# Pacing the conditioning projection of a two-layer hybrid transformer by stage instead of at one rate

## The chip, the cores and the metric

The kernel runs on one core of one Trainium2 chip. The metric is device time in microseconds, from the first to the last instruction with what lies around them. The median of 3 runs of the kernel before is 2766.06 us (2765.82 to 2766.23).

## The reference: what is computed

Two layers of a transformer backbone run over 512 latent tokens and 128 context tokens, which share all weights. Cut to what matters here, one layer is:

```python
sh1, sc1, gt1, sh2, sc2, gt2 = split(silu(c) @ w_mod[l] + b_mod[l], 6)      # adaLN: c for latents, c_ctx for context
h  = rmsnorm(x, norm1_g[l]) * (1 + sc1) + sh1
z  = h @ w_in[l] + b_in[l]                       # q, k, v of four mixers, and the branch gates
o  = [natten(z), dense_gqa(z), windowed_gqa(z), mlstm(z)]                   # mixers A, B, C, D
x  = x + gt1 * ((sum_i sigmoid(gate_i) * (o[i] @ w_branch[l, i])) @ w_out[l])
h2 = rmsnorm(x, norm2_g[l]) * (1 + sc2) + sh2
g, u = split(h2 @ w_ffn_in[l], 2)
x  = x + gt2 * ((silu(g) * u) @ w_ffn_out[l])
# after both layers: one final rmsnorm
```

D_MODEL is 1024, D_FF 2816. The adaLN projection `silu(c) @ w_mod[l]` has 6144 outputs for each of two conditioning vectors; `w_mod` is 25 MB for each layer.

## The kernel before, in words

**Tiling.** The 640 tokens lie side by side. `hT` holds the normed activations transposed, in two fp32r parts (high and low), and every float32 product is three TensorE matmuls: L414, L415, L416 in `mm3`, L1803 to L1805 in the paired part of the feed-forward. Weights come as 128x1024 blocks through SyncE's queue into two `raw` tiles (L397); ScalarE casts the high part `whi` (L402) and VectorE subtracts for the low part `wlo` (L403), into rings of five.

**Stages of a layer.** `mixers` runs projections and attention of A, D, B, C, and after each mixer its branch merge M0, M3, M1, M2 (`merge`, L1596 to L1610); while M2 runs (M20 to M23), no attention runs any more. Then come the output projection with its gated residual (`residual_tm`, L1631 and L1632), and, in `norm_tm`, the last two of its four column groups token tile by token tile, each followed by the next norm: sums of squares (L635 to L639), the root on GpSimd (L644), scaling (L649), TensorE transposes (L657), the modulation on ScalarE and VectorE, and the two parts of `hT` (L669, L670; the second half's low part on GpSimd). The feed-forward has four plain blocks (L1900, L1903) and then 18 paired ones (`ff_pair`), in four groups, each group followed by its output projection (`fo`) and residual. Group 3 ends in the norm of the next layer.

**The background.** Of the 24 column chunks of `w_mod` (12 for each layer, 512 columns each), `start` computes chunks 0 to 3 of layer 0 in the foreground, since the first norm needs them. The other 20 are the generator `adaln_all`. A chunk is eight accumulation steps: a 128x512 block of `w_mod` is loaded into one of four `wm` tiles (L497), VectorE multiplies and adds it into `msum` for the first vector (L477 for the first step, then L479), ScalarE multiplies it for the second (L473) and GpSimd adds that (L475; none in a chunk's first step). Then four transposes for each vector (L486) and a reduction (L487) give columns; for the chunks of the gates there is a second transpose (L516), a copy (L517) and a DMA to DRAM (L519).

**What sets the order.** Whenever a foreground generator has issued some matmuls, `run` or `drive` calls `tick`, which adds `bg[0]` to a credit and lets `adaln_all` go on for each whole step in it. `bg[0]` is `BGRATE` = 0.2 from the end of `start` to the end of the kernel. `bg_until` runs the rest of what is needed in one go where a stage needs certain chunks. The code order gives priorities; a scheduler then puts the instructions of each engine into one fixed order, by its own simulated times, and each engine executes its order strictly.

```python
    def tick():
        bg[1] += bg[0]
        bg_steps(int(bg[1]))
        bg[1] -= int(bg[1])
```

Of the kernel before, what the change touches and what calls it, by code (L numbers as in the profile page):

```python
# [86 lines left out]
BGRATE = 0.2  # L87
# [137 lines left out]
def trunk(ctx: ExitStack, tc: tile.TileContext, a: dict, depth: int):  # L225
    nc = tc.nc
# [240 lines left out]

    def adaln_acc(accs, w, kk, tmp=None):

        for v in range(2):  # L470
            s = csil[:, kk, v:v + 1]
            if v and tmp is not None:
                S.activation(accs[v][:, :512] if kk == 0 else tmp, w, AF.Copy, scale=s)  # L473
                if kk:
                    G.tensor_tensor(accs[v][:, :512], accs[v][:, :512], tmp, ALU.add)  # L475
            elif kk == 0:
                V.tensor_scalar(accs[v][:, :512], w, s, None, ALU.mult)  # L477
            else:
                V.scalar_tensor_tensor(accs[v][:, :512], w, s, accs[v][:, :512], ALU.mult, ALU.add)  # L479

# [10 lines left out]
    def adaln_all(items):  # L491


        def load(x):
            if x < KT * len(items):
                (l, ch), k = items[x // KT], x % KT
                SY.dma_start(wm_tiles[x % 4], a["w_mod"][l, P * k:P * k + P, 512 * ch:512 * ch + 512])  # L497

# [34 lines left out]
    def start():  # L533
# [49 lines left out]
        for x, ch in enumerate(order):  # L583
# [21 lines left out]
            for k in range(k0, k0 + 4):  # L605
                z = xT[k // 2][:, NTOK * (k % 2):NTOK * (k % 2) + NTOK]
                h = f640()
                for v, c0, c1 in ((0, 0, NS), (1, NS, NTOK)):
                    S.activation(h[:, c0:c1], z[:, c0:c1], AF.Identity, bias=modc[:, 1, v, k:k + 1],
                                 scale=modc[:, 0, v, k:k + 1])  # L610
                V.tensor_copy(hT[:, k, 0, :], h)
                V.tensor_tensor(hT[:, k, 1, :], h, hT[:, k, 0, :].bitcast(F32), ALU.subtract)
        for pl, t in held:
            pl.give(t)
        bigs.give(big)
        ms.give(*xT)
        bg[0] = BGRATE
# [1032 lines left out]
    def drive(bulk, streams):  # L1650
# [22 lines left out]
        for name, needs, rate, gen in bulk:  # L1673
            if any(n not in done for n in needs):
                flush()
# [17 lines left out]
    def mixers(l, d, *start):  # L1693
        done.clear()

# [145 lines left out]
    def layer(l, *start):  # L1841
# [20 lines left out]
        bg_until(l, *range(6, 10))  # L1862
        hook = norm_tm(xs, pieces, KT, mg_lhs, gts, ms, 1)
# [11 lines left out]
        for g, cnt in enumerate(FF_SPLIT):  # L1875
# [4 lines left out]
            for jx in range(cnt):  # L1880
# [13 lines left out]
                if j >= FF_PLAIN:  # L1894
                    run(ff_pair(ops, ff_load(l, j, spare, ts), at))
                    continue
# [17 lines left out]
                if j == FF_PLAIN - 1:  # L1914
                    for k in range(4):
                        split(hT[:, k, 0, HALF:], hT[:, k, 1, HALF:], s1[:, HALF * k:HALF * k + HALF])
                    qs.give(s1)
# [14 lines left out]
            if g < 3:  # L1932
                for n in range(4):
                    residual_tm(xs, fo(n), cnt, lhs, gts, n)
            else:
                pieces = {0: fo(0), 1: fo(1), **pieces}
                hook = norm_tm(xs, pieces, cnt, lhs, gts, ks, 0 if l + 1 < depth else None)
# [102 lines left out]
```

## Time and profile before

| | us | share of the span |
|---|---|---|
| median of 3 runs | 2766.06 | |
| the profiled execution (span 2761.6 us) | 2763.34 | |
| TensorE (PE) busy | 2677.5 | 97% |
| VectorE (DVE) busy | 2126.9 | 77% |
| ScalarE (ACT) busy | 1432.3 | 52% |
| GpSimd (POOL) busy | 743.1 | 27% |

Busy time is an average over stages. The rows further down take single stretches: a `--windows` row gives, for a stretch, its length, each engine's busy time and its count of instructions, the granted TensorE clock (1.00 is all of 2.4 GHz, 0.50 is 1.2 GHz), the share of the DMA engines and GB/s. A timeline row gives start, duration, engine, line, operation, output and input tiles, shapes and count; in brackets how long the engine sat idle before it and what ended that.

### The profile page before, as it was taken

How to read it: one execution, taken by the hardware profiler on the slowest of the kernel's cores; microseconds unless marked ns; L12 is line 12 of the kernel's file. 1: busy time of each engine (PE TensorE's matmuls, PEld its weight loads, DVE VectorE, ACT ScalarE, POOL GpSimd, SP SyncE). 2: the span in 40 equal slices, each digit the busy share in tenths (PEclk: the TensorE clock that was granted, in tenths of full speed). 3: DMA queues.
4: the chain of work that ended last, by engine and by line, in shares of the span. 5: the costliest groups of instructions: out<-in, count | busy, mean ns of one | idle time of the engine just before them, and what ended most of it. 6: DMA issues, size and time to landing. Idle time of an engine off the chain costs nothing.

```text
span 2761.6 us, 51944 instructions
## 1 busy us (share of the span) xinstructions
PE 2677.5 (97%) x19514; PEld 2626.9 (95%) x19514; DVE 2126.9 (77%) x4780; ACT 1432.3 (52%) x3298; POOL 743.1 (27%) x650
## 2 busy tenths in 40 slices
PE   7999999999999899999989999999999999999998
PEld 4998999999999899999989999999999999999998
DVE  7767768888973787888877867778888847586967
ACT  5865446666652543434458744456666535333433
POOL 2001112121142435365440101212112332243433
PEclk9999999999999999999999999999999999999999
DMA  8223323112243333333332323312122432222222
GB/s 286 91 87 115 97 79 98 47 56 79 62 124 114 100 111 104 92 108 108 96 118 90 124 89 114 93 56 77 56 75 66 123 123 70 92 77 85 81 93 73
DMA packets 123580, 264.28 MB, mean 96 GB/s; under 512 B 14193, under 2 KB 40145, under 8 KB 123329
## 3 DMA queue, kind: packets, MB, share of 16 engines
q1 hardware_dynamic: 123328, 260.97, 29.8%
q8 instruction: 153, 2.51, 0.4%
q14 instruction: 99, 0.80, 0.1%
HBM read 252.73 MB, written 7.95 MB: 94 GB/s over the span
## 4 chain that ended last, share of the span: by engine, by line
PE 76%; DVE 12%; ACT 4%; issue 4%; DMA 2%; POOL 2%; SPq 0%; DVEq 0%; POOLq 0%; ACTq 0%
PE acc L414 17%; PE acc L415 17%; PE acc L416 17%; PE acc L1803 3%; PE acc L1804 3%; PE acc L1805 3%; PE O L1224 2%; PE T L1214 2%; DVE msum L479 2%; DVE wlo L403 1%; PE O L1804 1%; PE O L1803 1%; PE O L1805 1%; DMA raw<-wflat 1%; DMA wm<-w_mod 1%
## 5 line engine op out<-in xcount | busy, mean ns | idle before, releaser
L414 PE MATMUL acc<-hT,whi 128*128 128x384 f32 (+1 forms) x2240 | 701.3, 315 | 21.0 <-DVE hT L669 9.5
L415 PE MATMUL acc<-hT,whi 128*128 128x384 f32 (+1 forms) x2240 | 700.8, 313 | 6.0 <-DVE hT L670 4.2
L416 PE MATMUL acc<-hT,wlo 128*128 128x256 f32 (+1 forms) x2240 | 696.6, 312 | 1.1 <-DVE wlo L403 1.1
L402 ACT CAST whi<-raw 128x512 fp32r<-128x512 f32 (+1 forms) x488 | 299.5, 619 | 403.1 <-PE acc L415 186.4
L403 DVE TENSOR_TENSOR wlo<-raw,whi 128x512 fp32r<-128x512 f32 (+1 forms) x488 | 373.2, 768 | 136.4 <-ACT whi L402 129.2
L414 PEld LDWEIGHTS acc<-hT,whi 128*128 128x128 f32 x2240 | 424.1, 190 | 27.9 <-DVE hT L669 10.6
L415 PEld LDWEIGHTS acc<-hT,whi 128*128 128x128 f32 x2240 | 425.2, 190 | 9.4 <-DVE hT L670 5.0
L416 PEld LDWEIGHTS acc<-hT,wlo 128*128 128x128 f32 x2240 | 424.5, 190 | 2.3 <-DVE wlo L403 1.3
L475 POOL TENSOR_TENSOR msum<-msum,mtmp 128x512 f32<-128x512 f32 x140 | 214.9, 1535 | 262.6 <-ACT msum L473 164.7
L1604 POOL TENSOR_TENSOR m<-m,f 128x256 f32<-128x256 f32 x96 | 100.1, 1046 | 521.9 <-DVE f L1602 319.7
L1632 POOL TENSOR_TENSOR big<-big,t 128x256 f32<-128x256 f32 x150 | 128.5, 866 | 248.3 <-DVE t L1631 239.7
L729 ACT CAST pth<-T 128x512 fp32r<-128x512 f32 (+1 forms) x232 | 118.1, 521 | 103.3 <-PE T L1214 58.2
L473 ACT ACTIVATE mtmp<-wm,csil 128x512 f32<-128x512 f32 x140 | 101.2, 723 | 127.5 <-POOL msum L475 123.2
L730 DVE TENSOR_TENSOR ptl<-T,pth 128x512 fp32r<-128x512 f32 (+1 forms) x232 | 137.1, 601 | 37.2 <-ACT pth L729 36.0
L1631 DVE TENSOR_TENSOR t<-acc,P 128x256 f32<-128x256 f32 x200 | 82.8, 419 | 107.6 <-PE acc L416 84.8
L451 ACT CAST whi<-of 128x512 fp32r<-128x512 f32 x144 | 88.9, 620 | 146.2 <-PE acc L1804 47.6
L414 PE MATMUL acc<-whi,m 128*128 128x256 f32 x560 | 158.3, 284 | 4.7 <-DVE t L1631 4.5
L414 PE MATMUL acc<-big,whi 128*128 128x256 f32 (+1 forms) x512 | 158.7, 311 | 2.7 <-ACT f L1596 2.6
L416 PE MATMUL acc<-whi,m 128*128 128x256 f32 x560 | 157.2, 281 | 1.7 <-DVE m L452 1.7
L415 PE MATMUL acc<-big,whi 128*128 128x256 f32 (+1 forms) x512 | 158.9, 311 | 0.0
L416 PE MATMUL acc<-big,wlo 128*128 128x256 f32 (+1 forms) x512 | 158.6, 310 | 0.0
L415 PE MATMUL acc<-wlo,m 128*128 128x256 f32 x560 | 157.2, 281 | 0.0
(464 smaller groups left out, 7905.9 us busy)
## 6 DMA issues: line engine op xcount, KB each, us to landing
raw<-wflat SPq DMA_DIRECT2D x236, 512.0 KB
wm<-w_mod SPq DMA_DIRECT2D x160, 256.0 KB
raw<-wflat SPq DMA_DIRECT2D x120, 256.0 KB
q<-wflat SPq DMA_DIRECT2D x48, 256.0 KB
kv<-nbias SPq DMA_DIRECT2D x16, 576.0 KB
kv<-mdr SPq DMA_DIRECT2D x16, 320.0 KB
big<-x_sample SPq DMA_DIRECT2D x8, 512.0 KB
P<-gt_d SPq DMA_DIRECT2D x32, 128.0 KB
```

Source lines behind the costliest of these rows:

```text
L402: S.copy(hi[:, :n], raw[:, s0:s0 + n])
L403: V.tensor_tensor(lo[:, :n], raw[:, s0:s0 + n], hi[:, :n].bitcast(F32), ALU.subtract)
L414: T.matmul(ps, lhs(k, 0), rhs(k, 0), start=(k == 0), stop=False)
L415: T.matmul(ps, lhs(k, 0), rhs(k, 1), start=False, stop=False)
L416: T.matmul(ps, lhs(k, 1), rhs(k, 0), start=False, stop=(k == kn - 1))
L475: G.tensor_tensor(accs[v][:, :512], accs[v][:, :512], tmp, ALU.add)
L729: S.copy(hi[:, :n], ps[:, :n])
L730: V.tensor_tensor(lo[:, :n], ps[:, :n], hi[:, :n].bitcast(F32), ALU.subtract)
L1632: (V if n == 3 else G).tensor_tensor(xs[tt][:, 256 * n:256 * n + 256], xs[tt][:, 256 * n:256 * n + 256], t[:, :256], ALU.add)
L1803: T.matmul(ps, f(0), ops[name](k, 0), start=first and k == 0, stop=False, **more)
L1804: T.matmul(ps, f(0), ops[name](k, 1), start=False, stop=False, **more)
L1805: T.matmul(ps, f(1), ops[name](k, 0), start=False, stop=k == 3, **more)
```

## The change

`BGRATE` goes. Each stage sets `bg[0]` itself: 0.14 in the mixers (`BG_MIX`), 0.8 from M20 until the norm (`BG_FREE`), 0 in `norm_tm` and through the plain feed-forward blocks that follow, 0.1 in the paired blocks (`BG_PAIR`), 0.3 in the output projections of groups 0 to 2 (`BG_OUT`), 0 again in the norm at the end of group 3. And a no-sync ordering edge is put on the first background load, the first ScalarE and the first VectorE instruction of a step: at the start behind the last modulation and the last `hT` instruction, and in each layer behind the split after the plain blocks. What is computed is the same.

```diff
-BGRATE = 0.2
+BG_MIX, BG_FREE, BG_PAIR, BG_OUT = 0.14, 0.8, 0.1, 0.3
...
+    def behind(eng):
+        if eng in bg_after:
+            after(newest(), bg_after.pop(eng), "the norm and what follows it go before the background")
...
                 S.activation(accs[v][:, :512] if kk == 0 else tmp, w, AF.Copy, scale=s)
+                behind("S")
...
+            if v == 0 and tmp is not None:
+                behind("V")
...
                     S.activation(h[:, c0:c1], z[:, c0:c1], AF.Identity, bias=modc[:, 1, v, k:k + 1],
                                  scale=modc[:, 0, v, k:k + 1])
+                    bg_after["S"] = newest()
                 V.tensor_copy(hT[:, k, 0, :], h)
                 V.tensor_tensor(hT[:, k, 1, :], h, hT[:, k, 0, :].bitcast(F32), ALU.subtract)
+                bg_after["V"] = newest()
+        bg_after["load"] = bg_after["S"]
...
-        bg[0] = BGRATE
+        bg[0] = BG_MIX
...
+            if name == "M20":
+                bg[0] = BG_FREE
...
         bg_until(l, *range(6, 10))
+        bg[0] = 0.0
         hook = norm_tm(xs, pieces, KT, mg_lhs, gts, ms, 1)
...
                 if j >= FF_PLAIN:
+                    bg[0] = BG_PAIR
...
             if g < 3:
+                bg[0] = BG_OUT
...
                 pieces = {0: fo(0), 1: fo(1), **pieces}
+                bg[0] = 0.0
```

The lines of the kernel after are numbered 2 to 27 higher. Three places show what this does to the fixed orders.

VectorE in the first norm of layer 0 (`start`); `hT` is what the first matmuls read, `modr` and `modc` are the modulation, `msum` is the background. Before:

```order
L612 TENSOR_TENSOR hT<-f_153,hT 128x640
L477 TENSOR_SCALAR msum_69<-wm_65,csil 128x512
L611 CAST hT<-f_151 128x640
L479 SCALAR_TENSOR_TENSOR msum_69<-wm_66,csil,msum_69 128x512
L612 TENSOR_TENSOR hT<-f_151,hT 128x640
L595 COPY of_7_444<-acc_162 2x512
L479 SCALAR_TENSOR_TENSOR msum_69<-wm_67,csil,msum_69 128x512
L599 COPY modr<-acc_163 128x8
L479 SCALAR_TENSOR_TENSOR msum_69<-wm_68,csil,msum_69 128x512
L627 TENSOR_TENSOR modc<-modr,sm 128x4 x2
```

After:

```order
L629 TENSOR_TENSOR hT<-f_153,hT 128x640
L628 CAST hT<-f_151 128x640
L629 TENSOR_TENSOR hT<-f_151,hT 128x640
L611 COPY of_7_444<-acc_162 2x512
L615 COPY modr<-acc_163 128x8
L646 TENSOR_TENSOR modc<-modr,sm 128x4 x2
L647 SCALAR_TENSOR_TENSOR modc<-modc,sm 128x4 x2
L628 CAST hT<-f_152 128x640
```

The four background instructions are gone from between; VectorE's first one now stands behind the last chunk of `hT`.

ScalarE at the same place; `mtmp` is the background's single scratch tile, which GpSimd must have added before ScalarE writes it again. Before:

```order
L609 ACTIVATE f_151<-m_2_206,modc 128x128
L473 ACTIVATE mtmp<-wm_66,csil 128x512
L473 ACTIVATE mtmp<-wm_67,csil 128x512
L473 ACTIVATE mtmp<-wm_68,csil 128x512
L609 ACTIVATE f_152<-m_3_207,modc 128x512
```

After:

```order
L485 ACTIVATE mtmp<-wm_66,csil 128x512
L625 ACTIVATE f_151<-m_2_206,modc 128x512
L625 ACTIVATE f_151<-m_2_206,modc 128x128
L625 ACTIVATE f_152<-m_3_207,modc 128x512
L625 ACTIVATE f_153<-m_3_207,modc 128x512
```

The modulation of the second half (`m_3`, `m_4`) now follows directly on the first; one background multiplication has moved ahead of it, in front of `m_2`, and waits for nothing on GpSimd.

GpSimd from the second norm of layer 0 on; L644 is the root of a norm, L670 a low part of `hT`, L1632 a residual add, L475 the background. Before:

```order
L1632 TENSOR_TENSOR big_6_9247<-big_6_9247,t_149 128x256
L670 TENSOR_TENSOR hT<-f_152,hT 128x4x128
L644 TENSOR_TENSOR sb_82<-ss_81,mhalf 128x1
L475 TENSOR_TENSOR msum_70<-msum_70,mtmp 128x512
L1632 TENSOR_TENSOR big_6_9247<-big_6_9247,t_148 128x256
L475 TENSOR_TENSOR msum_70<-msum_70,mtmp 128x512
L670 TENSOR_TENSOR hT<-f_151,hT 128x4x128
```

After:

```order
L1651 TENSOR_TENSOR big_6_9286<-big_6_9286,t_149 128x256
L689 TENSOR_TENSOR hT<-f_152,hT 128x4x128
L663 TENSOR_TENSOR sb_82<-ss_81,mhalf 128x1
L1651 TENSOR_TENSOR big_6_9286<-big_6_9286,t_148 128x256
L689 TENSOR_TENSOR hT<-f_151,hT 128x4x128
```

All 14 background adds of this norm have left it. Of the 140 adds, the stages of layer 0 (mixers to M1; M2; output projection and norm; feed-forward; norm of layer 1) held 42, 7, 14, 21, 7 before and hold 28, 28, 5, 30, 0 now; those of layer 1 (mixers; M2) held 35, 14 and hold 21, 28. The 5 stand ahead of the first root of the norm.

## Rows read from the trace of the kernel before

**Rows 1.** The page: busy time by engine, and the chain that ended last.

```profile
PE 2677.5 (97%) x19514; PEld 2626.9 (95%) x19514; DVE 2126.9 (77%) x4780; ACT 1432.3 (52%) x3298; POOL 743.1 (27%) x650
...
PE 76%; DVE 12%; ACT 4%; issue 4%; DMA 2%; POOL 2%; SPq 0%; DVEq 0%; POOLq 0%; ACTq 0%
```

**Rows 2.** Windows by stage: length; PE, PEld, DVE, ACT, POOL busy; clock; DMA.

```profile
881.00:1018.90 137.90, 125.12 (x925) 122.82 (x924) 104.93 (x187) 62.65 (x141) 55.36 (x46) 0.95 0.38 123
2250.80:2372.80 122.00, 119.67 (x915) 118.94 (x914) 79.82 (x163) 52.92 (x125) 31.12 (x32) 0.99 0.31 104
1018.90:1374.90 356.00, 351.23 (x2616) 350.12 (x2615) 294.16 (x433) 150.04 (x279) 173.40 (x133) 1.00 0.32 100
2372.80:2722.80 350.00, 348.36 (x2590) 347.22 (x2590) 260.61 (x400) 134.12 (x255) 133.81 (x112) 1.00 0.26 84
```

**Rows 3.** The same windows, instructions on `msum` alone (no ScalarE scratch).

```profile
881.00:1018.90 137.90, 2.07 (x16) 1.79 (x16) 18.02 (x16) 1.49 (x2) 23.46 (x14) 0.95 0.38 123
1018.90:1374.90 356.00, 3.87 (x25) 2.92 (x25) 25.92 (x24) 2.17 (x3) 34.12 (x21) 1.00 0.32 100
```

**Rows 4.** Timeline of PE, second norm of layer 0: its longest waits.

```profile
943.93 0.84 PE L414 MATMUL acc<-hT,whi 128*128 128x384 f32 x2 [2.54 <-DVE hT L669]
947.89 0.69 PE L415 MATMUL acc<-hT,whi 128*128 128x384 f32 x1 [3.12 <-DVE hT L670]
...
964.67 1.01 PE L414 MATMUL acc<-hT,whi 128*128 128x256 f32 x3 [3.49 <-DVE hT L669]
```

**Rows 5.** Windows inside the second norm, layer 0 and layer 1.

```profile
940.00:950.00 10.00, 4.34 (x21) 3.67 (x21) 10.00 (x20) 4.50 (x11) 5.42 (x5) 0.82 0.55 164
...
2320.00:2330.00 10.00, 7.67 (x49) 7.01 (x48) 8.36 (x20) 4.24 (x10) 1.29 (x1) 0.83 0.01 2
```

**Rows 6.** Timeline at the first norm: ScalarE, then PE.

```profile
46.22 0.72 ACT L473 ACTIVATE mtmp<-wm,csil 128x512 f32<-128x512 f32 x1 [1.40 <-POOL msum L475]
46.85 1.50 ACT L609 ACTIVATE f<-m,modc 128x512 f32<-128x512 f32 x2
...
50.04 1.11 PE L414 MATMUL acc<-hT,whi 128*128 128x256 f32 x3 [3.65 <-DVE hT L611]
51.68 0.58 PE L415 MATMUL acc<-hT,whi 128*128 128x256 f32 x1 [0.53 <-DVE hT L612]
...
58.75 0.39 PE L415 MATMUL acc<-hT,whi 128*128 128x256 f32 x1 [1.33 <-DVE hT L612]
```

**Rows 7.** Windows: the matmuls that follow those waits, and their clock.

```profile
50.04:56.20 6.16, 5.63 (x23) 5.16 (x24) 6.16 (x9) 3.98 (x9) 2.82 (x4) 0.56 0.36 96
```

**Rows 8.** Windows: the norm of layer 1 at the end of group 3.

```profile
1374.90:1385.00 10.10, 6.49 (x49) 5.87 (x48) 9.95 (x19) 4.13 (x7) 5.08 (x4) 0.91 0.40 124
1385.00:1395.00 10.00, 9.99 (x65) 9.78 (x65) 8.93 (x14) 3.59 (x10) 8.08 (x9) 0.75 0.45 143
...
1425.00:1435.00 10.00, 5.58 (x29) 4.85 (x29) 6.87 (x19) 8.05 (x28) 1.91 (x2) 0.80 0.55 169
```

**Rows 9.** Windows: mixers A to C, both layers; then one wait from PE's timeline.

```profile
71.10:789.20 718.10, 700.28 (x5138) 689.80 (x5137) 572.68 (x1576) 429.37 (x1058) 110.16 (x98) 1.00 0.27 83
1448.40:2160.90 712.50, 703.78 (x5154) 694.25 (x5153) 565.67 (x1575) 429.44 (x1054) 105.43 (x98) 1.00 0.27 84
...
229.53 1.02 PE L1310 MATMUL T<-ident,zif 128*16 128x128 f32 x4 [2.55 <-DVE grow L517]
```

**Rows 10.** Windows: stage M2 of layer 0 and its densest background in layer 1.

```profile
789.20:881.00 91.80, 91.80 (x634) 91.73 (x634) 48.10 (x75) 37.77 (x65) 26.95 (x24) 1.00 0.33 100
...
2175.00:2212.00 37.00, 37.00 (x263) 36.84 (x262) 35.28 (x41) 19.41 (x32) 24.73 (x19) 1.00 0.44 140
```

**Rows 11.** The same two stretches, instructions on `msum` alone.

```profile
789.20:881.00 91.80, 0.87 (x5) 0.64 (x5) 7.12 (x8) 0.73 (x1) 10.40 (x7) 1.00 0.33 100
2175.00:2212.00 37.00, 1.20 (x8) 1.00 (x8) 13.97 (x12) 1.11 (x2) 18.46 (x12) 1.00 0.44 140
```

More of the change, by code (lines that the diff above doesn't have):

```diff
@@ L466, in mod_slice, with newest @@
         return modr[:, w, s, 4 * (ch % 2):4 * (ch % 2) + 4, :]
+    bg_after = {}
+    def newest():
+        return list(nc.cur_bb.bb.instructions)[-1]
+    def behind(eng):
+        if eng in bg_after:
+            after(newest(), bg_after.pop(eng), "the norm and what follows it go before the background")
     def adaln_acc(accs, w, kk, tmp=None):
@@ L497, in load @@
                 SY.dma_start(wm_tiles[x % 4], a["w_mod"][l, P * k:P * k + P, 512 * ch:512 * ch + 512])
+                behind("load")
         load(0)
@@ L1694, in mixers @@
         done.clear()
+        bg[0] = BG_MIX
         def mg(i, jj, needs=(), rate=0.0):
@@ L1916, in layer @@
                         split(hT[:, k, 0, HALF:], hT[:, k, 1, HALF:], s1[:, HALF * k:HALF * k + HALF])
+                    bg_after.update(dict.fromkeys(("load", "S", "V"), newest()))
                     qs.give(s1)
```

## The prediction

> **What bounds the kernel now.** I began with the page. TensorE is busy for 2677.5 us of 2761.6, and it holds 76% of the chain that ended last [rows 1]. So 84.1 us are all that the end can come earlier by keeping TensorE fed, plus what a lowered clock costs, and neither an unburdened VectorE nor an unburdened GpSimd is worth anything by itself. The background (adaLN) matters only where it stands in front of something that TensorE waits for.
>
> Then I went along TensorE's timeline by waits, and cut the span into the same stages of both layers, because the code of the two is the same and the background is not. Output projection and second norm, up to the first paired block, take 137.9 us in layer 0 and 122.0 in layer 1 [rows 2]. In layer 0, 16 accumulation steps lie in that stretch, with 18.02 us of VectorE and 23.46 of GpSimd [rows 3]; by the orders layer 1 has none left behind its M2. TensorE waits there up to 3.49 us at a time for `hT` from VectorE [rows 4], VectorE is busy for 10.00 of 10 us where TensorE gets 4.34, and the clock is 0.82; in layer 1 the worst ten microseconds still have TensorE at 7.67 [rows 5]. The reader is to see that VectorE, with 77% over the span, is the limit in single stretches only, and that the background sits in them. The same picture, smaller, is at the first norm [rows 6, 7] and at the norm of layer 1 [rows 8].
>
> **The change part by part.** Nothing is added to or removed from the work: 160 steps before and after. They move, and I cost each place that they leave or enter, against the profiled execution's 2763.3 us.
>
> *Second norm of layer 0: 14 us less.* All 14 adds of GpSimd leave the norm; 5 come back ahead of its first root, beside the output projection. The stretch of layer 1 is the model for what is left: 137.9 - 122.0 = 15.9 us is the most [rows 2]. TensorE's transposes of the background don't vanish (2.07 us for 16 [rows 3]), so I take 14. If the 5 adds that remain of 14 kept their share, 15.9 x 9 / 14 = 10.2: the other end.
>
> *First norm: 6.5 us less.* ScalarE's modulation of the second half starts at 46.85, directly behind a background multiplication that waited 1.40 us for GpSimd [rows 6]; four VectorE steps stand between `hT`, `modr` and `modc` as well. TensorE then waits 3.65 + 0.53 + 1.33 = 5.51 us [rows 6], and works the following 6.16 us at a clock of 0.56, that is mostly at 1.2 GHz: 5.63 us of matmuls that would take 5.63 x 0.56 = 3.2 at 2.4 GHz, so 2.4 more [rows 7]. Together 7.9 at most. What comes last then is the norm's own chain through ScalarE and VectorE, so not all of it; I take 6.5, and 3.0 (a little over half of the waits) as the other end. The eight steps themselves move behind the norm, beside matmuls that no longer wait.
>
> *Norm of layer 1 in group 3: 5 us less.* Its 7 adds fall to none. TensorE loses 10.10 - 6.49 = 3.6 us in the first ten, while VectorE is busy 9.95, and the next ten run at 0.75, which costs 2.5: 6.1 [rows 8]. The hole at the end, 4.4 us from 1425 on, comes when VectorE has room (6.87 of 10) and is the norm's own latency; I leave it. Without the early backlog VectorE may still be near full with this norm's four residuals, so 5, with ends of 2.5 and 9 (some of the late hole too).
>
> *Mixers: 6 us less.* Their adds fall from 42 to 28 and from 35 to 21, 14 in each layer, which is 16 steps (seven adds to eight steps). No row shows mixers without the background. The nearest price is the feed-forward: 356.0 us with 24 steps against 350.0 with none, 0.25 us a step [rows 2, 3]. That makes 4 us for each layer. For layer 0 I keep 4, since its mixers leave 718.1 - 700.28 = 17.8 us of TensorE unused and one wait of 2.55 ends with the background's own copy (L517) [rows 9]; for layer 1, with 8.7 unused, I take 2. Ends: 0, since an order that changes can put other waits in place of these, and 12.
>
> *Feed-forward of layer 0: 2.5 us more.* Its adds rise from 21 to 30, some 10 steps; at 0.25 us each, 2.5. Ends: 0 (they stand under paired matmuls) and 5.
>
> *M2, where most of it goes: nothing.* It gets 28 adds in each layer instead of 7 and 14, so 32 steps. The cover is the gate and branch matmuls, with VectorE busy for 48.10 of 91.8 us and GpSimd for 26.95 [rows 10]. In the dense piece of layer 1, 12 steps lie in 37 us, and TensorE is busy for 37.00 of them [rows 10, 11]; 32 in 91.8 us are 12.9 in 37, hardly denser. A step cost VectorE 13.97 / 12 = 1.16 us there, so layer 0 would come to 48.10 - 7.12 + 32 x 1.16 = 78.1 us of 91.8 [rows 10, 11]. SyncE's queue carries 32 loads of 256 KB among the weights; a `wm` load that waits for its tile holds the weight loads behind it. In the dense piece the same was so at 140 GB/s, without a wait of TensorE. I take 0, and as the other end the 0.25 us of the feed-forward for the 24 and 16 steps more: 10.
>
> The sum: -14 - 6.5 - 5 - 6 + 2.5 + 0 = -29. 2763.3 - 29 = 2734.3; the median of the runs stands 2.7 above the profiled execution, so 2737 us. All good ends give -45 and 2721, all bad ones -0.7 and 2765.
>
> A row that speaks about crowding: one background step costs VectorE 1.16 us in the dense piece and 18.02 / 16 = 1.13 in the norm [rows 3, 11], much of it waiting inside the instruction. The Trainium skill's page "SBUF — State Buffer" (section "SBUF: two separate sides") says that GpSimd and a VectorE instruction with two SBUF inputs take a port pair by an exclusive lock, and that the loser blocks for the whole instruction. That speaks against putting GpSimd's adds close together, and what it would make here is the first rival.
>
> **The rivals.** *M2 becomes VectorE's stage (slower).* If each of the 28 adds (18.46 / 12 = 1.54 us [rows 11]) kept VectorE standing for its whole length on top of the 1.16, VectorE would need 78.1 + 28 x 1.54 = 121 us for 91.8, and the stage would grow by 29 us in layer 0 and about as much in layer 1: 2737 + 58 = 2795. It decides from (91.8 - 78.1) / 28 = 0.5 us for an add; from 1.0 us for an add on, the two layers lose 2 x 14.3 = 29, and the kernel is no faster than before. Against it: in the dense piece VectorE was busy 35.28 us of 37 with 12 adds of 18.46 us beside it, and TensorE lost nothing [rows 10]; the standing is inside the durations that I summed. By the skill's rule the standing is real, and the trace agrees that it exists, but not that it comes on top. 6%.
>
> *The order gives part of it back.* The scheduler makes a new order for everything; waits as those of rows 9 (2.55 us) turn up at other places, four of them and no gain in the mixers: -29 + 6 + 10 = -13, 2753. For it: layer 0 leaves 9 us more of TensorE unused in its mixers than layer 1 at the same 40 steps, so 10 us come from order alone [rows 9]. 22%.
>
> *The second norm of layer 0 is slow for another reason* than the background (its input, its clock): then 14 falls to about 4, and the time is 2747. Against it: VectorE's surplus over layer 1 is 104.93 - 79.82 = 25.1 us, of which 18.02 are the background itself [rows 2, 3]. 7%.
>
> That the change doesn't do what it says is excluded by the orders: GpSimd's shows no background in either norm.
>
> **How the numbers follow.** The forecast, 2737 with its own 2727 to 2747, has 60%; the given-back order 22%, the other cause 7%, the crowded M2 6%, and 5% are for more than I sum (2721 to 2727). The range runs from 2726 to 2757, which leaves out the crowded M2, part of the given-back order and of the best case. A measurement can tell about 0.2%, 5.5 us, from no change: under 2760.5 lie the forecast, most of the given-back order and of the other cause and the better one, 88%; within, 6%; slower than 2771.6, the crowded M2, 6%.
>
> **What would show it.** In the trace after: no L475 between the roots of either norm; output projection and second norm of layer 0 near 124 us with TensorE's waits for `hT` under 2 us; no wait near 50 us and no clock of 0.56 there; the first twenty microseconds of the last residual of layer 0 with TensorE over 9 of 10; M2 with TensorE busy throughout; TensorE's unused time near 60 us instead of 84. It would be wrong if VectorE reaches all of M2 and matmuls there wait for `wlo` or gates, if weights come late behind `wm` loads, or if the second norm of layer 0 stays near 138 us.

## The result and the profile after

The median after is 2730.49 us (2728.15 to 2732.18) against 2765.94 (2761.98 to 2766.23) in the same session: ratio 0.9877, interval 0.9864 to 0.9890, 35 us less. The forecast was 2737 with a range of 2726 to 2757.

Each stage is taken from the first matmul of its kind in the trace to the first of the next, in the profiled executions; "sum" is what the prediction put there. "Output projection and second norm" runs up to the first paired block and so holds the four plain blocks; "feed-forward" runs from there to the residual of its last group, and the norm of layer 1 from there to the first product of mixer A.

| stage | before | after | change | sum |
|---|---|---|---|---|
| start, to the first product of mixer A | 71.1 | 65.1 | -6.0 | -6.5 |
| mixers and M2, layer 0 | 809.9 | 802.1 | -7.8 | -4 |
| output projection and second norm, layer 0 | 137.8 | 122.8 | -15.0 | -14 |
| feed-forward, layer 0 | 356.0 | 368.0 | **+12.0** | **+2.5** |
| norm of layer 1 | 73.5 | 62.7 | -10.8 | -5 |
| mixers and M2, layer 1 | 802.3 | 797.9 | -4.4 | -2 |
| output projection and second norm, layer 1 | 122.0 | 119.2 | -2.8 | 0 |
| feed-forward, layer 1 | 350.0 | 349.7 | -0.3 | 0 |

The total was near because the misses had opposite signs, which is luck: 9.5 us too little was put on the feed-forward of layer 0, and 5.8 too little was taken off at the norm of layer 1, 6.2 in the mixers with M2 and 3.8 in the two second norms. The page of after answers to [rows 1]: TensorE's unused time is 2726.4 - 2665.0 = 61.4 us where it was 84.1. Its busy time fell too, by 12.5 us for the same 19514 matmuls, with a mean granted clock of 0.996 where it was 0.991.

```profile
PE 2665.0 (98%) x19514; PEld 2618.7 (96%) x19514; DVE 2125.9 (78%) x4780; ACT 1434.3 (53%) x3298; POOL 732.1 (27%) x650
...
PE 81%; DVE 10%; ACT 3%; issue 3%; DMA 2%; POOL 1%; DVEq 0%; SPq 0%; POOLq 0%; ACTq 0%
```

The windows of after, columns as in [rows 2]. The first four answer to [rows 2] (output projection and norm of both layers, feed-forward of both); then M2 of layer 0, as [rows 10]; the start, where the clock is back at 1.00 (0.56 in [rows 7]); the whole norm of layer 1; and, inside the feed-forward of layer 0, its second group, the paired blocks of that group and the worst eight microseconds.

```profile
867.30:990.10 122.80, 119.28 (x915) 117.62 (x914) 91.72 (x178) 58.93 (x136) 45.03 (x42) 1.00 0.38 126
2218.60:2337.80 119.20, 117.40 (x910) 116.80 (x910) 80.90 (x165) 51.99 (x125) 31.41 (x33) 1.00 0.31 107
990.10:1358.10 368.00, 356.48 (x2623) 353.46 (x2622) 308.22 (x448) 155.52 (x289) 186.82 (x142) 0.99 0.33 104
2337.80:2687.50 349.70, 348.14 (x2591) 347.27 (x2590) 258.34 (x400) 134.44 (x255) 133.68 (x112) 1.00 0.26 84
...
767.40:867.30 99.90, 99.90 (x699) 99.50 (x698) 81.44 (x108) 51.42 (x87) 52.48 (x42) 1.00 0.46 145
...
50.00:56.00 6.00, 5.02 (x28) 4.31 (x28) 5.87 (x9) 4.60 (x16) 3.01 (x2) 1.00 0.36 105
...
1358.10:1420.80 62.70, 57.10 (x431) 55.62 (x430) 48.03 (x104) 36.61 (x107) 24.38 (x29) 0.97 0.33 109
...
1134.20:1262.70 128.50, 121.34 (x884) 120.19 (x883) 110.88 (x155) 54.06 (x101) 70.61 (x53) 0.97 0.34 108
...
1186.00:1262.70 76.70, 71.19 (x470) 70.43 (x470) 72.57 (x98) 36.85 (x72) 37.23 (x25) 0.96 0.34 109
...
1190.00:1198.00 8.00, 4.82 (x18) 4.82 (x19) 8.00 (x10) 2.44 (x5) 3.45 (x3) 0.58 0.47 139
```

M2 has TensorE busy for all of its 99.90 us, with VectorE at 81.44. It is longer than before's 91.80 since 699 matmuls stand in it instead of 634; that is why the table takes mixers and M2 together. In before, the norm of layer 1 and the same group of the feed-forward, which took 118.9 us, were:

```profile
1374.90:1448.40 73.50, 62.51 (x437) 59.50 (x436) 59.22 (x116) 41.12 (x114) 35.53 (x36) 0.91 0.38 122
...
1161.60:1280.50 118.90, 117.20 (x875) 116.79 (x874) 101.06 (x145) 49.68 (x93) 59.58 (x46) 1.00 0.32 99
```

TensorE's timeline of after at the first norm, the rows with a wait for `hT` (compare [rows 6]: 3.65, 0.53 and 1.33):

```profile
47.33 0.39 PE L417 MATMUL acc<-hT,whi 128*128 128x256 f32 x1 [0.73 <-DVE hT L629]
...
50.41 0.39 PE L417 MATMUL acc<-hT,whi 128*128 128x256 f32 x1 [0.36 <-DVE hT L629]
...
51.90 0.67 PE L416 MATMUL acc<-hT,whi 128*128 128x256 f32 x3 [0.41 <-DVE hT L628]
...
52.76 0.39 PE L417 MATMUL acc<-hT,whi 128*128 128x256 f32 x1 [0.19 <-DVE hT L629]
```

and at the second norm of layer 0 (compare [rows 4]: 2.54, 3.12 and 3.49), now as long as in layer 1:

```profile
942.41 0.62 PE L416 MATMUL acc<-hT,whi 128*128 128x256 f32 x3 [1.50 <-DVE hT L688]
943.33 0.39 PE L417 MATMUL acc<-hT,whi 128*128 128x256 f32 x1 [0.30 <-DVE hT L689]
```

**Where the 12 us of the feed-forward went.** Eight background steps stand between 1180 and 1200 us, where a group's output projection gives way to its first paired block (TensorE's first paired product is at 1180.41 us). TensorE's longest wait of the stage is there:

```profile
1193.18 0.64 PE L1825 MATMUL acc<-hT,whi 128*128 128x320 f32 x1 [3.86 <-DVE f L1843]
```

VectorE's timeline of the same stretch follows. None of its rows from 1180 to 1200 us has an idle time in brackets: it is never idle there, and `f` (L1843), for which TensorE waits, stands behind an `msum` of 1.75 us.

```profile
1181.26 1.78 DVE L454 TENSOR_TENSOR wlo<-of,whi 128x512 fp32r<-128x512 f32 x1
...
1183.57 0.41 DVE L1650 TENSOR_TENSOR t<-acc,P 128x256 f32<-128x256 f32 x1
...
1188.04 0.68 DVE L454 TENSOR_TENSOR wlo<-of,whi 128x512 fp32r<-128x512 f32 x1
1188.64 0.74 DVE L492 SCALAR_TENSOR_TENSOR msum<-wm,csil,msum 128x512 f32<-128x512 f32 x1
1189.30 0.48 DVE L1839 TENSOR_TENSOR f<-acc,f 128x320 f32<-128x320 f32 x1
1189.70 1.35 DVE L454 TENSOR_TENSOR wlo<-q,whi 128x512 fp32r<-128x512 f32 x1
1190.98 1.75 DVE L492 SCALAR_TENSOR_TENSOR msum<-wm,csil,msum 128x512 f32<-128x512 f32 x1
1192.65 0.48 DVE L1843 TENSOR_TENSOR f<-acc,f 128x320 f32<-128x320 f32 x1
```

ScalarE at the same time stands idle for the scratch tile that GpSimd has not yet added, with the casts of the paired blocks behind it (after the first such wait comes `whi`):

```profile
1187.87 0.73 ACT L485 ACTIVATE mtmp<-wm,csil 128x512 f32<-128x512 f32 x1 [3.23 <-POOL msum L488]
1188.50 0.61 ACT L453 CAST whi<-raw 128x512 fp32r<-128x512 f32 x1
...
1192.21 0.72 ACT L485 ACTIVATE mtmp<-wm,csil 128x512 f32<-128x512 f32 x1 [2.06 <-POOL msum L488]
```

So there were three suspects for the loss: the number of steps, that eight are drawn together (a burst), and what they stand beside; and two for the engine: VectorE without room, or ScalarE behind GpSimd.

### The profile page after: what moved, and what is told of

It reads as the page before. It is cut to its first block, busy times and chain, and to the rows that moved or that the text cites. A ratio compares the mean times of both kernels' runs of the same rounds, so it can differ in the third digit from the quotient of the medians.

```text
span 2726.4 us, 51965 instructions
## 1 busy us (share of the span) xinstructions
PE 2665.0 (98%) x19514; PEld 2618.7 (96%) x19514; DVE 2125.9 (78%) x4780; ACT 1434.3 (53%) x3298; POOL 732.1 (27%) x650
## 4 chain that ended last, share of the span: by engine, by line
PE 81%; DVE 10%; ACT 3%; issue 3%; DMA 2%; POOL 1%; DVEq 0%; SPq 0%; POOLq 0%; ACTq 0%
PE acc L416 18%; PE acc L417 18%; PE acc L418 18%; PE acc L1825 3%; PE acc L1826 3%; PE acc L1827 3%; PE O L1243 2%; PE T L1233 2%; DVE msum L492 1%; PE O L1826 1%; PE O L1825 1%; PE O L1827 1%; DVE wlo L405 1%; DMA wm<-w_mod 1%; PE S L1200 1%
## 5 line engine op out<-in xcount | busy, mean ns | idle before, releaser
L416 PE MATMUL acc<-hT,whi 128*128 128x256 f32 (+1 forms) x2240 | 698.0, 313 | 11.6 <-DVE hT L688 5.6
L417 PE MATMUL acc<-hT,whi 128*128 128x256 f32 (+1 forms) x2240 | 696.7, 311 | 2.3 <-DVE hT L629 1.3
L488 POOL TENSOR_TENSOR msum<-msum,mtmp 128x512 f32<-128x512 f32 x140 | 206.7, 1476 | 227.4 <-ACT msum L485 133.1
L748 ACT CAST pth<-T 128x512 fp32r<-128x512 f32 (+1 forms) x232 | 117.9, 520 | 112.2 <-PE T L1233 53.9
L485 ACT ACTIVATE mtmp<-wm,csil 128x512 f32<-128x512 f32 x140 | 101.4, 724 | 127.6 <-POOL msum L488 114.9
```

Of the source, the lines that this page charges most:

```text
L416: T.matmul(ps, lhs(k, 0), rhs(k, 0), start=(k == 0), stop=False)
L417: T.matmul(ps, lhs(k, 0), rhs(k, 1), start=False, stop=False)
L748: S.copy(hi[:, :n], ps[:, :n])
```

## The experiments

Each was timed for three rounds or five beside the kernel before (2763.5 to 2764.8 us in these sessions). The stages are cut as above (mixers and M2 of a layer together; "norm 2" holds the output projection and "ff 0" is the feed-forward of layer 0). They come from one execution of each version, while the medians come from four to ten.

| | us | ratio, interval | start | mixers 0 | norm 2, layer 0 | ff 0 | norm, layer 1 | mixers 1 |
|---|---|---|---|---|---|---|---|---|
| after | 2730.5 | 0.9877 (0.9864, 0.9890) | 65.1 | 802.1 | 122.8 | 368.0 | 62.7 | 797.9 |
| e1 | 2732.6 | 0.9887 (0.9872, 0.9901) | 71.2 | 798.8 | 124.0 | 368.7 | 64.2 | 798.0 |
| e2 | 2740.9 | 0.9914 (0.9899, 0.9929) | 65.1 | 802.0 | 123.0 | 357.8 | 74.5 | 807.3 |
| e3 | 2714.2 | 0.9818 (0.9803, 0.9832) | 64.8 | 793.6 | 127.2 | 361.6 | 61.2 | 795.3 |
| e4 | 2692.4 | 0.9737 (0.9721, 0.9753) | 63.3 | 792.3 | 122.1 | 350.0 | 63.9 | 791.5 |
| e5 | 2723.4 | 0.9849 (0.9832, 0.9865) | 64.9 | 797.4 | 119.6 | 364.1 | 70.8 | 795.0 |
| e6 | 2711.0 | 0.9804 (0.9789, 0.9818) | 64.5 | 806.9 | 121.4 | 350.0 | 64.0 | 795.5 |
| e7 | 2793.0 | 1.0100 (1.0085, 1.0115) | 65.0 | 799.6 | 118.7 | 412.2 | 62.5 | 803.7 |
| e8 | 2749.0 | 0.9950 (0.9936, 0.9964) | 64.6 | 810.1 | 128.2 | 369.8 | 61.1 | 806.4 |
| e9 | 2704.1 | 0.9789 (0.9776, 0.9803) | 64.5 | 799.2 | 121.2 | 352.2 | 64.8 | 792.7 |
| e10 | 2708.0 | 0.9796 (0.9779, 0.9812) | 64.3 | 794.5 | 126.1 | 356.7 | 62.6 | 791.7 |
| e11 | 2773.1 | 1.0029 (1.0019, 1.0038) | 67.0 | 815.7 | 123.4 | 371.7 | 62.5 | 817.7 |
| e12 | 2706.5 | 0.9792 (0.9778, 0.9805) | 67.0 | 794.4 | 120.8 | 353.2 | 66.3 | 794.7 |

**e4, the floor: no steps.** All but one of the 160 steps and their loads are left out, so what they compute is missing; the transposes and reductions stay.

```diff
         load(0)
-        load(1)
...
-                adaln_acc(msum, wm_tiles[(KT * i + k) % 4], k, mtmp)
-                load(KT * i + k + 2)
+                if i == 0 and k == 0:
+                    adaln_acc(msum, wm_tiles[0], 0, mtmp)
```

> The changed kernel without 159 of the 160 accumulation steps and their loads (the conditioning from the background is not computed; transposes, reductions and everything else stay). It gives the floor. Theory (M2 hides its 32 steps, the feed-forward and the mixers pay for theirs): M2 of both layers as long as in the changed kernel within 1 us, feed-forward of layer 0 at 349 to 352, mixers of both layers together 4 to 10 us shorter, in all 2700 to 2708. Rival (the steps that are left cost nothing, what differs is order): 2720 to 2728. Second rival (M2 pays for its crowd): M2 shorter by 3 us or more in each layer.

It went lower than any of its cases. What the steps and their loads still cost after is 2726.4 - 2690.2 = 36 us of the profiled spans: 18.0 in the feed-forward of layer 0, 9.8 and 6.4 in the mixers with M2, 1.8 at the start, next to nothing in the norms. M2 alone takes 97.3 us in layer 0 and 100.0 in layer 1 without steps, 99.8 and 96.7 in after with 30 and 24. The single lengths go with the matmuls that the order puts there (684, 701, 699 and 671); the two layers together take 197.3 us without steps and 196.5 with 54, so M2 hides them.

**e1, without the edges at the start; e2, without the pace in the paired blocks.**

```diff
-        bg_after["load"] = bg_after["S"]
+        bg_after.clear()
```

> The changed kernel without the ordering edges at the first norm; everything behind the first norm stands in the same order. Theory (stage by stage: each stage that the background left keeps its own gain to the end): the 6 us that the first norm gained come back, 2736 to 2738 us, with TensorE's wait of about 3.6 us near 50 us and the low clock after it as before the change, and every later stage as long as in the changed kernel. Rival (TensorE's later stages have slack that swallows an early start): within 2 us of the changed kernel, 2729 to 2733.

The start is 6.1 us longer, near the 6.5 that was put, and the wait of [rows 6] is back, 3.64 us where it was 3.65:

```profile
49.97 0.68 PE L416 MATMUL acc<-hT,whi 128*128 128x256 f32 x3 [3.64 <-DVE hT L628]
```

But mixers and M2 of layer 0 are 3.3 us shorter. In after the eight steps run at the end of the start and the beginning of mixer A (VectorE's from 53.9 to 66 us, GpSimd's adds up to 75), and TensorE has two waits there that e1 does not have (after, 40 to 75 us: in all, times, longest):

```profile
PE S L952 <- DVE m L742: 1.4, 1, 1.4
...
PE S L951 <- DVE sa L956: 0.8, 1, 0.8
```

So about half of what the first norm gains is paid where the eight steps go. In the total the two kernels can't be told apart: e1's 2732.6 us lies in the rival's range, although its profiled execution is 5.8 us longer than that of after.

```diff
-BG_MIX, BG_FREE, BG_PAIR, BG_OUT = 0.14, 0.8, 0.1, 0.3
+BG_MIX, BG_FREE, BG_PAIR, BG_OUT = 0.14, 0.8, 0.0, 0.3
```

> The changed kernel with the rate 0 in the paired feed-forward blocks; the steps that are then missing are forced into the norm of layer 1, whose GpSimd order holds 7 background adds again, as before the change. Theory (the feed-forward of layer 0 lost 12 us by the 8 steps that stand together in one paired block): the feed-forward of layer 0 falls from 368 to 356 to 359 us, the norm of layer 1 (from its end on to the first attention product, 62.6 us now) rises by 8 to 11 us, in all 2727 to 2734. Rival (the feed-forward lost by the higher rate in its output projections, or by its new order as such): it stays at 366 to 369, the norm still rises, 2738 to 2743.

The group of 128.5 us is back at 118.5 with one burst of eight less, and the feed-forward falls by 10.2, as the theory said. The total went the other way, into the rival's range: the eight steps landed in the norm of layer 1, which is 11.8 us longer with them, and mixers and M2 of layer 1 are 9.4 us longer, which neither case had. Those stages hold 54 steps instead of 56, and TensorE is idle in them for 13.4 us instead of 7.1: a new order can cost that much without a step more.

```profile
1134.20:1252.70 118.50, 116.81 (x872) 116.40 (x871) 100.29 (x145) 49.20 (x92) 59.79 (x46) 1.00 0.31 98
```

**e3, e5: every step pinned.** Each background step gets an ordering edge behind the foreground instruction issued just before it, so that the scheduler cannot pull it forward; e3 with the pace of after, e5 with 0.2 at every stage as before.

```diff
         while n > 0 and bg[2]:
+            bg_after.update(dict.fromkeys(("load", "S", "V"), newest()))
             if next(bg[2][0], None) is None:
```

> The changed kernel with an ordering edge on every background step instead of at two places: each step's load, ScalarE and VectorE instruction is put behind the last foreground instruction that the program has issued by then, so that the scheduler can't pull eight steps together. Rates as in the changed kernel; neither norm holds a background add. Theory (bursts are what costs): feed-forward of layer 0 at 355 to 359 us instead of 368, mixers as they are within 4 us, in all 2717 to 2723. Rival (steps cost by their number, about 0.25 us each, wherever they stand): feed-forward at 364 to 369, in all 2727 to 2734.

> The kernel of e3 (an ordering edge that pins every background step behind the foreground instruction that was issued just before it) with the old pace: 0.2 a step at every stage, norms and paired blocks included. Theory (what costs is that the scheduler draws the steps of a chunk together; spread evenly they cost little anywhere, even in the norms): mixers and M2 of layer 0 together 794 to 797 us, feed-forward of layer 0 360 to 364, norm of layer 1 64 to 70, second norm of layer 0 with its output projection 124 to 131, total 2715 to 2723. Rival (the pace by stage is what counts, edges are a side matter): the norms are hit again, norm of layer 1 at 70 us or more, second norm of layer 0 at 132 or more, total 2735 to 2745.

e3 is 16 us faster than after, under its theory's total, by 8.5 us in mixers and M2 of layer 0 and 6.4 in the feed-forward; its second norm of layer 0 is 4.4 longer. The feed-forward fell between theory and rival. e5 says more: at before's single pace, pinning alone gives 41 us, more than the change with its paces by stage and edges at three places. Its mixers of layer 0 hold 42 steps in 703.6 us, before's held 40 in 718.0. But its feed-forward, with the steps spread, still takes 364.1: drawing together cannot be the whole cost there. The norm of layer 1, where ten steps stand again, takes 70.8 us instead of 62.7, as e5's rival had it.

**e7, e6, e9: where the steps stand.** e7 is after with the pace of the mixers in M2; e6 and e9 are e3 with other paces: e6 0.3 in the mixers of layer 0 and none in its feed-forward, e9 between e3 and e6.

```diff
# e7
-BG_MIX, BG_FREE, BG_PAIR, BG_OUT = 0.14, 0.8, 0.1, 0.3
+BG_MIX, BG_FREE, BG_PAIR, BG_OUT = 0.14, 0.14, 0.1, 0.3
# e6, then e9 (BG_MIX by layer; 0.2 from the output projection on)
+BG_MIX, BG_FREE, BG_PAIR, BG_OUT = (0.3, 0.14), 0.8, 0.0, 0.0
+BG_MIX, BG_FREE, BG_PAIR, BG_OUT = (0.2, 0.14), 0.8, 0.08, 0.2
```

> The kernel after with BG_FREE = 0.14 instead of 0.8, so that M2 is paced like the mixers and holds 7 adds in layer 0 instead of 28; by the order about 12 of the rest come to stand in the plain blocks and about 30 in the paired blocks of layer 0, drawn together, none in the two norms. Theory (M2 hides its steps for nothing, and the paired blocks pay for drawn-together steps some 2.5 us a burst of eight and more where bursts follow each other): M2 of layer 0 at most 3 us shorter than after's 99.8, feed-forward of layer 0 380 us or more against 368.0, total 2740 to 2755. Rival (M2's steps cost there what they cost elsewhere, so that it does not matter where they go): M2 of layer 0 5 us shorter or more, feed-forward at most 375, total within 5 us of after's 2730.5.

> The edges of e3 on every step and a pace of its own: 0.3 a step in the mixers of layer 0, 0.14 in those of layer 1, 0.8 in M2, 0.2 from the output projection on, none in the norms, none in the whole feed-forward of layer 0 but what stands in the plain blocks of layer 1. Theory (a step pinned beside matmuls of the mixers or of M2 costs next to nothing, steps beside paired blocks cost what e3 still shows over 350 us): feed-forward of layer 0 350 to 351 us, output projection and second norm of layer 0 122 to 124, mixers and M2 of layer 0 together 794 to 800, total 2700 to 2706. Rival (steps cost by their number, wherever they stand): the 11 us that the feed-forward gives up come back in the mixers and M2 of layer 0, 804 us or more there, total 2711 to 2716.

> The edges of e3 on every step, with the steps put where the runs so far gave a low price: about 42 in the mixers of layer 0 (0.2 a step; e5 paid 8.6 us over the floor of e4 for as many), as many as e6 in M2 (0.8), 0.2 beside the output projection, about 20 in the feed-forward of layer 0 (0.08 and 0.2) instead of 31 or none, none in the norms, layer 1 as in e3 and e6. Theory (the price of a step rises with how many stand in a stage, about 0.1 us each for the first 30 in a layer's mixers, 0.5 for the next 30, 0.4 each in the feed-forward, so the middle is cheapest): mixers of layer 0 701 to 704 us, feed-forward 356 to 359, total 2705 to 2710, under e6's 2711.0 and e3's 2714.2. Rival (a constant price for each step, so that the split does not matter): total 2711 to 2715.

e7 went 38 us beyond its theory. M2 of layer 0 is 1.2 us shorter with 16 steps instead of 30; the feed-forward with 55 steps is 62 us over the floor, and that of layer 1, where 15 came to stand, 19. In e6 the rival was right: mixers and M2 of layer 0 are at 806.9, so that the 63 steps in its mixers cost 14.6 us over the floor, 0.23 each, while e3's 31 cost 1.3. e9 came 1 us under the range of its total; its feed-forward, 352.2, was better than its theory.

These runs let the feed-forward's steps be counted by what they stand beside (from 3 us ahead of a group's first gated product of `residual_tm` to 2 us behind its last, against the rest, paired or plain blocks):

| | beside an output projection | beside blocks | us over e4's 350.0 |
|---|---|---|---|
| before | 24 | 0 | 6.0 |
| e2 | 24 | 1 | 7.8 |
| e9 | 20 | 2 | 2.2 |
| e3 | 23 | 8 | 11.6 |
| e5 | 20 | 10 | 14.1 |
| after | 24 | 9 | 18.0 |
| e7 | 17 | 38 | 62.2 |

Beside an output projection a step costs 0.1 us (e9, pinned) to 0.25 (before, not pinned). Beside blocks it costs 1.2 to 1.5, after what the first column takes is deducted (after: (18.0 - 6.0) / 9 = 1.3; e5, at 0.1 for the others: 12.1 / 10; e7, at 0.25: 58 / 38), whether single (e5) or in a burst (after); at 0.25 for the others, e5's would still be 0.9. How the two places differ is seen in windows of before, layer 1, where no step is: output projection of a group, then its paired blocks.

```profile
2397.30:2441.00 43.70, 43.42 (x368) 43.21 (x367) 21.45 (x41) 9.18 (x16) 16.34 (x19) 1.00 0.23 71
2441.00:2513.60 72.60, 72.60 (x500) 72.60 (x500) 67.66 (x93) 34.99 (x70) 30.03 (x21) 1.00 0.29 89
```

VectorE is busy for 49% of the first and 93% of the second: 5 us are free in 72.6, room for four steps. (ScalarE is busier too, 48% against 21%.) The forecast's 0.25 us came from the row of before, whose 24 steps all stand in the first kind. In e7 VectorE is full and TensorE waits for it:

```profile
1080.00:1160.00 80.00, 61.42 (x372) 59.58 (x370) 79.20 (x93) 35.94 (x67) 50.75 (x35) 0.89 0.34 113
```

and by e7's waits of TensorE in the feed-forward (us in all, times, longest) it is `f` again:

```profile
PE acc L1825 <- DVE f L1843: 22.7, 8, 6.8
PE S L501 <- DVE msum L492: 6.3, 1, 6.3
```

where e9 has, in the whole of its own:

```profile
PE acc L1826 <- DVE f L1844: 1.4, 1, 1.4
PE acc L422 <- DVE t L1651: 0.8, 3, 0.3
```

**e8, e10, e11: which engine.** On e3, a step without VectorE (both products on ScalarE, both sums on GpSimd), and on VectorE alone; on after, two scratch tiles.

```diff
# e8
-        for v in range(2):
+        for v in ((1, 0) if tmp is not None else (0, 1)):
...
-            if v and tmp is not None:
-                S.activation(accs[v][:, :512] if kk == 0 else tmp, w, AF.Copy, scale=s)
+            if tmp is not None:
+                prod = accs[v][:, :512] if kk == 0 else tmp if v else w
+                S.activation(prod, w, AF.Copy, scale=s)
...
-                    G.tensor_tensor(accs[v][:, :512], accs[v][:, :512], tmp, ALU.add)
+                    G.tensor_tensor(accs[v][:, :512], accs[v][:, :512], prod, ALU.add)
...
# e10
...
-                adaln_acc(msum, wm_tiles[(KT * i + k) % 4], k, mtmp)
+                adaln_acc(msum, wm_tiles[(KT * i + k) % 4], k)
# e11
...
-    wm_tiles = [cp.tile([P, 512], F32, name=f"wm{i}") for i in range(4)]
-    mtmp = cp.tile([P, 512], F32, name="mtmp")
+    wm_tiles = [cp.tile([P, 512], F32, name=f"wm{i}") for i in range(3)]
+    mtmp = [cp.tile([P, 512], F32, name=f"mtmp{i}") for i in range(2)]
...
```

> The kernel of e3, but VectorE has no part in a step: both vectors are multiplied on ScalarE and added on GpSimd (for the first vector the product is written in place into the wm tile). The steps stand where e3 has them, 31 of them in the feed-forward of layer 0. VectorE gives up 160 instructions of about 1.1 us, ScalarE gets 160 of 0.7 and GpSimd 140 of 1.5 us more. Theory (a step beside paired blocks costs because VectorE, which feeds every block with f and wlo, has no room for its 1.1 us): feed-forward of layer 0 352 to 356 us against e3's 361.6, mixers and M2 of layer 0 together 790 to 794, total 2698 to 2707. Rival (GpSimd's adds hold VectorE, or the loads and matmuls of the background cost): feed-forward 362 us or more, total 2712 to 2730.

> The kernel of e3, but a step is two VectorE instructions: ScalarE and GpSimd have no part in it. VectorE gets 160 instructions of 0.74 us more (118 us); against that, by the sums of e3 and e4, it no longer stands beside 140 adds of GpSimd (its other instructions take 62 us less in e4, and its own 160 would fall from 1.03 us to 0.74, another 46), so that it comes out 10 us above e3; ScalarE no longer waits for the scratch tile (88 us in e3). Theory (what delays TensorE is ScalarE standing behind GpSimd for the scratch tile, and GpSimd holding VectorE): feed-forward of layer 0 352 to 357 us against e3's 361.6, total 2698 to 2708. Rival (it is the instructions that VectorE has to fit in, whatever their length): feed-forward 362 us or more, total 2716 to 2735.

> The kernel after with two scratch tiles for ScalarE's product in place of one (the room is taken from the ring of w_mod tiles, three instead of four); the steps stand in the same stages, drawn together as before. In after, ScalarE waits 114.9 us in all for GpSimd to free the scratch tile, 3.23 and 2.06 us of it in the burst at 1180 to 1200 us. Theory (these waits make ScalarE's casts late and so the paired blocks): the second group of paired blocks 121 to 124 us against 128.5, feed-forward of layer 0 360 to 364 against 368.0, total 2714 to 2724. Rival (VectorE, busy throughout the burst, is what is late): feed-forward 366 to 369, total 2726 to 2734.

e8 is 35 us slower than e3, beyond its rival's range, though VectorE is busy for 2051.9 us instead of 2136.7. TensorE still waits for `f`, and VectorE now waits 18.0 us for GpSimd's residual adds (2.4 in e3). The feed-forward of layer 0 in e8, waits of TensorE, then of VectorE:

```profile
PE acc L1824 <- DVE f L1842: 9.3, 5, 4.0
...
DVE t L1649 <- POOL big L1650: 18.0, 12, 2.8
```

The durations of VectorE's records tell why so little came of it: without the `msum` steps they sum to 2167.7 us in e4, 2229.6 in e3 and 2293.8 in e8. So a background add of GpSimd makes VectorE's other instructions longer by 62 / 140 = 0.44 us in e3 and 126 / 280 = 0.45 in e8; in e10, which has no such add and 320 `msum` instructions, the sum is 2161.5, so it is the adds that do it. The price depends on where they stand: in e9 it is (2209.4 - 2167.7) / 140 = 0.30. That GpSimd's foreground work stands in the same order as the adds (the `big` row) is the other part; how the 35 us divide was not separated.

e10 hit its theory in the feed-forward (356.7) and at the edge in the total: 6 us faster than e3, with VectorE as busy as there (306.33 us of the feed-forward against 306.12, 2134.9 of the whole against 2136.7). The same steps at the same places cost 6.7 us over the floor instead of 11.6. So VectorE's room is not the whole price of a step either; ScalarE's standing, GpSimd's adds or both are part of it, and which of the two was not separated. A third path, ScalarE's wait for the weight sums that GpSimd makes for the paired blocks (`of`), is no suspect: it is 6.6 us in the feed-forward of e4 without any step and 8.2 in after.

e11 answered neither way, because the room for the second scratch tile came out of the `w_mod` ring. ScalarE's waits for the scratch fell from 114.9 to 52.2 us in all, and a wait for loads took their place (waits of ScalarE in e11, whole span):

```profile
ACT mtmp L485 <- DMA wm<-w_mod: 84.1, 46, 8.2
...
ACT mtmp L485 <- POOL msum L488: 52.2, 38, 4.5
```

M2 of layer 0 is 111.7 us there, 12 longer than after. Three tiles are too few for a dense M2; a second scratch tile beside four was not tried.

**e12, e9's placing with e10's step.**

> The steps placed and pinned as in e9, each made of two VectorE instructions as in e10, with no part of ScalarE or GpSimd; some 22 steps in the feed-forward of layer 0, so 44 instructions of VectorE. Theory (the two gains add: e10 took 6 us from e3, and e9 another 10 by the placing): the mixers and M2 of both layers together 3 to 6 us less than e9's 991.9 + 799.2 would leave (that is, their sum over both layers at 1786 to 1789), feed-forward of layer 0 351 to 353, total 2697 to 2702. Rival (e9 has left nothing that a step's other engines still cost, and VectorE's longer own time comes on top): total 2703 to 2708.

(The mixers' sums in this text are added wrongly: e9's are 799.2 and 792.7, 1591.9 together, and 3 to 6 less would have been 1586 to 1589.) They came to 794.4 + 794.7 = 1589.1, but the start, the feed-forward and the norms of layer 1 are some 7 us longer together, and the total is the rival's: the same as e9 within the intervals. With the steps placed as in e9 it did not matter which engine made them. e9 at 2704.1 us is the fastest version that computes everything: 26 us under the change (0.9789 against 0.9877 of before).

## Why the prediction was right, and where it was not

- **Second norm of layer 0: right.** 14 put, 15.0 measured, with the mechanism of [rows 3 to 5], though nine adds and not five are left in the stretch, all ahead of the norm's first root: the window above has VectorE at 91.72 us instead of 104.93, and TensorE's longest wait for `hT` is 1.50 us instead of 3.49 [rows 4]. The model (layer 1, [rows 2]) was itself 3 us too long; it fell to 119.2 although no step stood in it before or after.
- **First norm: right at its place, half of it given back.** 6.5 put, 6.0 measured. The step that failed is the sentence that the eight steps move "beside matmuls that no longer wait": the comparison with e1 shows 3.3 us there, 2.2 of it in two new waits.
- **Norm of layer 1: undersized.** 5 put, 10.8 measured, beyond the bound of 9. The failed step is that only the first twenty microseconds were costed and the rest was left as "the norm's own latency". In after TensorE's idle time in this norm is 5.6 us instead of 11.0, and its busy time 57.10 us instead of 62.51, at a clock of 0.97 instead of 0.91; the 2.5 us put for the clock covered ten microseconds only. The late hole is smaller, not gone: TensorE still waits 2.6 us for `hT` there. e2, with eight steps back in the norm, has 74.5 us again, so the steps are what costs.
- **Mixers: undersized, 12.2 with M2 against 6, just past the end of 12.** The price of 0.25 us a step was a guess from another stage. By mixers and M2 of layer 0 over the floor, it is not a constant: 0.04 us for each of the 31 pinned steps in e3's mixers, 0.12 for e5's 42, 0.23 for e6's 63. Those that were not pinned cost more, 17.6 / 40 = 0.44 in before and 9.8 / 25 = 0.39 in after.
- **M2 for nothing: right.** TensorE is never idle in it in layer 0 (96.46 of 96.70 us in layer 1), and e4 and e7 move it by at most 3 us in layer 0. VectorE's 81.44 of 99.90 us is near the estimate of 78.1 of 91.8. The first rival (M2 becomes VectorE's stage) did not happen, and e8's 0.45 us for an add is under the 0.5 from which it would decide; the durations that were summed hold most of it already.
- **Feed-forward of layer 0: the mis-sized term.** 2.5 put, 12.0 measured, outside its ends of 0 and 5. The failed step is the price, and with it "they stand under paired matmuls": the 0.25 us was measured where VectorE is half idle, and the new steps went where it is 93% busy. Estimated afterwards from the place itself, the burst of eight (seven adds) brings VectorE about 8 x 1.13 [rows 3] + 7 x 0.44 = 12 us of work into some 5 us of free time, 7 us too much; TensorE's idle time in that group rose by 7.2 - 1.7 = 5.5 us, before what the clock adds. The size fits, but it proves nothing: VectorE has no gap from 1180 to 1226 us, yet 4.1 us are left in the paired blocks of the group (72.57 of 76.70), and e10 shows that more than VectorE's room counts. That these steps cost the 10 us is shown by e2; through which engine stays open.
- **The rival that the order gives back 13** did not come true in the mixers of after. A loss of that kind came in the feed-forward (the 3.86 us wait), and e2 shows one in the mixers of layer 1, 9.4 us with two steps fewer.
- **The rival that the second norm is slow for another reason** is out: the stretch fell to 122.8 us, and e4, without any step, has 122.1.

## What to carry to other kernels

Price background work by the free time, in the very stretch it enters, of the engine it needs, not by an average over the stage: the same step cost 0.1 to 0.25 us beside an output projection and 1.2 to 1.5 beside a paired block. Free time of one engine is not all of it: e10 filled VectorE as much as e3 and was faster, with no background add on GpSimd. A pace in the program is only a wish as long as the scheduler may pull the steps forward; pinning each step behind its neighbour was worth more here than all the paces together. And a test that moves background out of one place always puts it into another: read all stages before calling it a loss or a gain.

## What the runs showed of the hardware

A GpSimd add costs VectorE time even where neither waits for the other by a semaphore. In the burst above the same `wlo` takes 0.68 us alone and 1.78 while a GpSimd add runs, and over the whole of after `wlo<-of,whi` has a mean of 0.68 us in 112 records without a GpSimd instruction of over 0.9 us beside it (for more than 0.1 us) and 1.20 in 32 with one. An instruction that reads its first operand from `acc`, `t<-acc,P`, is 0.42 us in both cases (151 and 49). GpSimd's rows of the stretch:

```profile
1181.02 1.47 POOL L488 TENSOR_TENSOR msum<-msum,mtmp 128x512 f32<-128x512 f32 x1
...
1190.47 1.71 POOL L488 TENSOR_TENSOR msum<-msum,mtmp 128x512 f32<-128x512 f32 x1
```

The Trainium skill's page "SBUF — State Buffer" (section "SBUF: two separate sides") gives the rule for it, that a VectorE instruction with two SBUF inputs and a GpSimd instruction that reads SBUF exclude each other, and the trace agrees, with the 0.68 and 1.20 us above. Its page "Perfetto Trace Analysis" (section "Optimizing Scalar/DVE Operations") warns that moving work between these two might not help; e8 agrees, with 0.45 us of VectorE's time for each GpSimd add and a total 35 us worse.

A stall cost more here than its wait: in the second group of after TensorE is idle 128.50 - 121.34 = 7.2 us against 1.7 before, and its busy time is 4.1 us longer. Of these, 1.5 us are transposes of the background (2.68 us in this group against 1.20); the rest goes with a clock of 0.97 instead of 1.00 (0.58 in the worst eight microseconds, between the two levels of 1.2 and 2.4 GHz).
